# Value products and modulation steps that start with their last operand, and experts turned in pairs

## The chip, the cores and the metric

The kernel runs as one program on one core of a Trainium2 chip. The time is the device time of one execution in microseconds (us). TensorE (PE in the profile) multiplies, VectorE (DVE) and ScalarE (ACT) work elementwise, GpSimd (POOL) helps with a few small operations, and SyncE (SP) issues all DMAs on one queue. Each engine takes its instructions in the order in which they stand in its program.

## The reference, cut to what matters

Two transformer layers over 256 latent and 256 context tokens, with D = 1024. Each layer has a modulation, four attention branches and a channel mixer. Layer 0 has a dense SwiGLU, layer 1 eight experts of which each token takes two:

```
m = silu(cond) @ w_mod[l] + b_mod[l]                 # shift, scale and gate of both halves of a layer
p = softmax(q @ k.T * scale);  out = p @ v           # branches a, b, d; c subtracts two softmaxes
for each expert e and its tokens t:
    y[t] += w[t, e] * ((silu(h[t] @ w1[e]) * (h[t] @ w3[e])) @ w2[e])
x = x + m_gate * y
```

## The kernel before

**Layout.** Activations lie feature-major. Matrices are split into a float32r high and low part and multiplied in three float32r passes (`mm3`, L280). Plain float32 products also occur; each of these is two instructions in the trace. Three kinds of product use only part of TensorE's 128 columns at a time and put several results beside each other in different columns.

**Modulation (L310).** `mod_group` handles one of 40 background steps. It loads four tiles of `wmod`, then issues eight float32 products of 32 columns each: for k = 0 the four column groups g = 0 to 3, then for k = 1 the same. The last tile to land, `w[3]`, is read by k = 1, g = 2 and 3. In the trace a step is 16 instructions, L317.

**Value products (L625 to L632).** In the branches a, b and d a pair of heads gets its scores, an Exp, a division and transposes (L613); ScalarE copies the transposes into `both[0]` and `both[1]` (L615). Then `o[64j:64j+64]` sums V times `both[j]` over the key blocks, j = 0 before j = 1, each in 64 of the 128 columns. `turned` is the last of the copies, that of `both[1]`. There are 36 such products: 24 with four key blocks (16 instructions in the trace) and 12 with two (8 instructions), all L630.

**Experts (L1323 to L1346).** Per expert there are seven chunks of 512 hidden features. `gate_up` (L1410) multiplies up to 96 gathered tokens with four pieces of 1 MB each, in 72 products of 32 columns (`acc<-wraw,xg`, L1405 to L1408); ScalarE and VectorE form silu(gate)*up in the tile `ga`. `turn` (L1433) transposes it in three instructions (L1438) and copies it to `aT`. `down` (L1443) multiplies `aT` with two more pieces into `S` (36 products). The loop issues gate_up of chunk c, down of chunk c-1, turn of chunk c. At each expert's second chunk `selection` (L1224) makes a weighted selection matrix in two VectorE instructions, two transposes (L1231) and a copy. After the next expert's first chunk `weigh` (L1243) copies the expert's result to `ysb`, and `combine` (L1258) multiplies it with the weighted selection in eight float32 products (L1266, 16 instructions); VectorE adds these to the sum (L1355). Every second expert `gather` (L1234) collects tokens for two experts.

**Loading.** `pieces` (L1365) lists the 336 pieces in the order of use. They rotate through 8 + 5 + 4 = 17 buffers (`R1`, `R2` and two tiles that were `hh` and `hl`). A buffer is loaded again when its last product is done.

**Order.** The order on each engine is set by a scheduler that plays the program through with its own estimates of durations (L1622). It puts next on an engine what it holds to be ready. `issue_after(x)` puts those instructions of a block that run on x's own engine behind x; around the value products x is a ScalarE copy, and the block holds TensorE products alone.

Of the kernel before, what the change touches and what calls it, by code (L numbers as in the profile page):

```python
# [10 lines left out]
F32 = mybir.dt.float32  # L11
# [35 lines left out]
class Prog:  # L47
# [262 lines left out]
    def mod_group(self, l, G, s):  # L310

        nc = self.nc
        ps = self.acc()
        w = self.wloads(self.I["wmod"][l, 4 * G + s], 2048, self.mod_ring)
        for k in range(2):
            for g in range(4):
                nc.tensor.matmul(ps[32 * g:32 * g + 32, 0:256], self.sc[:, 2 * s + k, :],  # L317
                                 w[2 * k + g // 2][:, 256 * (g % 2):256 * (g % 2) + 256], start=k == 0, stop=k == 1)
# [252 lines left out]
    def attn_pair(self, qts, keys, smm, br, V, sink=None, mask=False, diff=False):  # L571


        nc = self.nc
        k0, nk = keys
        n = 128 * nk
        nq = len(qts)
        c0 = 128 * qts[0]
        hi, lo = br[0][:, c0:c0 + 128 * nq], br[1][:, c0:c0 + 128 * nq]
        oall = self.acc("tp") if diff else None  # L580
        both = None if diff else [self.at.tile([128, 4, 256], F32, name="PT2", tag="PT", bufs=self.PTB)[:, :nk] for _ in range(2)]
        for qi, qt in enumerate(qts):
            st = self.sm.tile([128, 8], F32, name="st", tag="st", bufs=6)
            P = []
            for j in range(2):
                S = self.acc("S")[:, :n]
                smm(S, j, qt)
                if mask and qt < 2:
                    ob = slice(128, 256) if qt == 0 else slice(0, 128)
                    nc.vector.tensor_tensor(S[:, ob], S[:, ob], self.amask[qt], op=OP.add)  # L590
                nm = st[:, j:j + 1]
                nc.vector.tensor_reduce(nm, S, axis=AX.X, op=OP.max, negate=True)
                if sink is not None:
                    nc.vector.tensor_scalar(nm, nm, self.nsink[:, sink + j:sink + j + 1], None, op0=OP.min)
                p = self.at.tile([128, 512], F32, name="P", tag="P", bufs=self.PB)[:, :n]
                nc.scalar.activation(p, S, AF.Exp, bias=nm, accum_out=st[:, 2 + j:3 + j])
                P.append(p)
            if sink is not None:
                nc.gpsimd.tensor_tensor(st[:, 4:6], self.sink[:, sink:sink + 2], st[:, 0:2], op=OP.add)
                nc.scalar.activation(st[:, 4:6], st[:, 4:6], AF.Exp)  # L600
                nc.vector.tensor_tensor(st[:, 2:4], st[:, 2:4], st[:, 4:6], op=OP.add)
            nc.vector.reciprocal(st[:, 2:4], st[:, 2:4])
            if diff:
                nc.vector.tensor_scalar(P[1], P[1], st[:, 3:4], self.lam, op0=OP.mult, op1=OP.mult)
                nc.vector.scalar_tensor_tensor(P[0], P[0], st[:, 2:3], P[1], op0=OP.mult, op1=OP.subtract)
            else:
                for j in range(2):
                    nc.vector.tensor_scalar(P[j], P[j], st[:, 2 + j:3 + j], None, op0=OP.mult)
            PT = []
            for j in range(1 if diff else 2):  # L610
                tp = self.acc("tp")
                for kc in range(nk):
                    nc.tensor.transpose(tp[:, 128 * kc:128 * kc + 128], P[j][:, 128 * kc:128 * kc + 128], self.ident)  # L613
                if not diff:
                    turned = nc.scalar.copy(both[j][:, :, 128 * qi:128 * qi + 128], tp[:, :n].rearrange("p (k t) -> p k t", t=128))  # L615
                    continue
                pt = self.at.tile([128, 4, 256], F32, name="PT", tag="PT", bufs=self.PTB).rearrange("p k t -> p (k t)")[:, :n]
                self.evac(pt, tp[:, :n])
                PT.append(pt)
            if diff:  # L620
                for kc in range(nk):
                    self.last_pv = nc.tensor.matmul(oall[:, 128 * qi:128 * qi + 128], PT[0][:, 128 * kc:128 * kc + 128],
                                     V(k0 // 128 + kc, 0), start=kc == 0, stop=kc == nk - 1)
                continue
        if not diff:  # L625
            o = self.acc("tp")[:, :128 * nq]
            with self.tc.issue_after(turned.ins):
                for kc in range(nk):
                    for j in range(2):
                        nc.tensor.matmul(o[64 * j:64 * j + 64], V(k0 // 128 + kc, j), both[j][:, kc, :],  # L630
                                         start=kc == 0, stop=kc == nk - 1)
# [592 lines left out]
    def selection(self, selT, pos, w, n=CAP):  # L1224
# [6 lines left out]
            nc.tensor.transpose(tp[0:n, 128 * t:128 * t + 128], sw, self.ident)  # L1231
        nc.scalar.copy(selT, tp[0:n, 0:256])

    def gather(self, htok, sel, n, put):  # L1234

        for k in range(KC):
# [21 lines left out]
    def combine(self, part, put):  # L1258

        nc = self.nc  # L1260
        ysb, selT = part
        for i in range(4):
            c = self.acc("tp")
            for j in range(2):
                dc = 2 * i + j
                nc.tensor.matmul(c[:, 256 * j:256 * j + 256], ysb[:, 128 * dc:128 * dc + 128], selT, start=True, stop=True)  # L1266
            put(i, c.rearrange("p (j t) -> p j t", j=2))

    def moe(self, x, close):
# [4 lines left out]
        with self.pool("epm") as self.ep:  # L1274
            with self.tc.issue_after(self.last_pow.ins):
                self.route_consts()
            R1, R2 = 8, 5
            self.loaded = []
            self.order = self.pieces()
            self.rings = [(self.ep, "wraw", R1, 1)] * R1  # L1280
# [6 lines left out]
            with self.pool("spm", side="right") as self.ex:  # L1287
# [16 lines left out]

                def chosen(e):

                    sel = self.ex.tile([128, 2, 2, CAP], F32R, name="sel", tag="sel", bufs=1)
# [11 lines left out]
                    return xg  # L1319

                xg = chosen(0)
                prev = None
                for e in range(NE):  # L1323
                    if e and e % 2 == 0:
                        xg = nxt
                    for c in range(7):
                        with self.tc.issue_after(self.last_tok.ins) if e == 0 else nullcontext():
                            a = self.gate_up(xg, CAP * (e % 2))
                            if prev:
                                self.down(*prev)  # L1330
                            prev = c, self.turn(a)
                            if e == 0 and c == 1:
                                rest()
                        if c == 0 and e:
                            self.combine(self.weigh(self.y, selT), lambda i, v: self.add_to(macc, i, v, e == 1))
# [5 lines left out]
                self.down(*prev)  # L1341
# [23 lines left out]
    def pieces(self):  # L1365


        out, prev = [], None
        for e in range(NE):
            for c in range(7):  # L1370
                out += [self.I["w13"][e, c, h] for h in range(4)]
                if prev:
                    out += [self.I["w2"][prev[0], prev[1], h] for h in range(2)]
                prev = e, c
        return out + [self.I["w2"][prev[0], prev[1], h] for h in range(2)]

    def load_next(self):

# [31 lines left out]
    def gate_up(self, xg, c0):  # L1410
# [9 lines left out]
        a = self.ex.tile([128, MAIN], F32, name="ga", tag="ga", bufs=2)  # L1420
# [12 lines left out]
    def turn(self, a):  # L1433
# [5 lines left out]
        aT = self.ex.tile([128, 3, 128], F32, name="aT", tag="aT", bufs=2)  # L1439
# [187 lines left out]
```

## Time and profile before

| | |
|---|---|
| median of 3 runs | 2608.15 us (2607.58 to 2610.31) |
| the profiled execution's own time | 2609.64 us |
| its span, first to last instruction | 2607.9 us |
| TensorE busy | 2564.9 us, 98% |
| VectorE, ScalarE, GpSimd busy | 46%, 36%, 4% |
| mean granted TensorE clock | 0.993 of full speed |
| experts, about 1623 us to the end | DMA moves 340 to 400 GB/s |

Busy time counts a column group that works alone as busy too, so a busy TensorE can still be working with half of its columns. Whether it does is seen in the timeline: what one start is later than the last.

### The profile page before, as it was taken

To read this page: it belongs to the slowest core of one execution; us is meant where nothing else is said; L and a number is where in the kernel's file an instruction comes from. 1 tells how busy PE (TensorE), PEld (TensorE's weight loads), DVE (VectorE), ACT (ScalarE), POOL (GpSimd) and SP (SyncE) were. 2 spreads that over 40 slices of the span, in tenths; PEclk is the share of its full clock that TensorE was granted. 3 is DMA by queue.
4 is the path that set the end of the run, shared out by engine and by line. 5 is a ranking of instruction groups with operands and counts; after the bars stand their busy time and mean duration, and the time that the engine had idled before them with its cause. 6 is when DMAs were issued, how large, how long until landed. Compare 5 with 4: busy or idle time off the path is not lost.

```text
span 2607.9 us, 54549 instructions
## 1 busy us (share of the span) xinstructions
PE 2564.9 (98%) x22762; PEld 1986.3 (76%) x22762; DVE 1212.5 (46%) x2820; ACT 929.6 (36%) x2179; POOL 116.5 (4%) x118
## 2 busy tenths in 40 slices
PE   8999999999999999999999999999999999999998
PEld 6866788898788778888888998666666666666665
DVE  6767666557574434458777786111112121211121
ACT  4556556444443323336666664111111111111111
POOL 0111010000000000001210001000000000000000
PEclk9999999999999999999999999999999999999999
DMA  6423321222352352345442457998898999898992
GB/s 239 130 72 94 107 90 65 82 75 91 97 170 69 110 173 95 89 128 173 148 130 86 138 160 293 405 393 353 342 378 350 362 363 378 359 359 350 397 360 81
DMA packets 153467, 543.22 MB, mean 208 GB/s; under 512 B 17920, under 2 KB 25216, under 8 KB 109696
## 3 DMA queue, kind: packets, MB, share of 16 engines
q1 hardware_dynamic: 153216, 539.68, 56.6%
q8 instruction: 181, 2.97, 0.4%
q14 instruction: 70, 0.57, 0.1%
HBM read 538.57 MB, written 1.05 MB: 207 GB/s over the span
## 4 chain that ended last, share of the span: by engine, by line


## 5 line engine op out<-in xcount | busy, mean ns | idle before, releaser
L1405 PE MATMUL acc<-wraw,xg 128*32 128x384 f32 x5376 | 606.8, 487 | 0.0
L1406 PE MATMUL acc<-wraw,xg 128*32 128x256 f32 x1792 | 471.8, 380 | 0.0
L260 ACT CAST whi<-wraw 128x512 fp32r<-128x512 f32 (+2 forms) x484 | 293.0, 608 | 453.8 <-PE acc L283 261.8
L261 DVE TENSOR_TENSOR wlo<-wraw,whi 128x512 fp32r<-128x512 f32 (+2 forms) x484 | 323.7, 672 | 275.1 <-ACT whi L260 267.6
L1429 DVE SCALAR_TENSOR_TENSOR ga<-ga,acc 96x192 f32<-96x192 f32 x224 | 79.6, 355 | 670.8 <-ACT ga L1427 666.5
L1405 PE MATMUL S<-wraw,aT 128*32 128x384 f32 x2688 | 306.3, 486 | 0.6 <-ACT aT L1440 0.6
L1405 PEld LDWEIGHTS acc<-wraw,xg 128*32 128x32 f32 x5376 | 224.1, 110 | 73.1 <-issue 12.0
L1427 ACT ACTIVATE ga<-acc 96x192 f32<-96x192 f32 x224 | 72.9, 326 | 547.5 <-PE acc L1408 544.9
L1408 PE MATMUL acc<-wraw,xg 128*32 128x256 f32 x896 | 266.5, 379 | 0.0
L1406 PE MATMUL S<-wraw,aT 128*32 128x256 f32 x896 | 239.2, 379 | 0.0
L1406 PEld LDWEIGHTS acc<-wraw,xg 128*32 128x32 f32 x1792 | 190.7, 110 | 59.2
L283 PE MATMUL acc<-wlo,hh 128*128 128x256 f32 (+1 forms) x752 | 212.6, 284 | 0.0
L284 PE MATMUL acc<-whi,hl 128*128 128x256 f32 (+1 forms) x752 | 212.1, 284 | 0.0
L282 PE MATMUL acc<-whi,hh 128*128 128x256 f32 (+1 forms) x752 | 210.9, 284 | 0.1
L282 PE MATMUL acc<-hh,whi 128*128 128x256 f32 (+1 forms) x616 | 209.2, 341 | 0.6 <-DVE tg L882 0.6
L284 PE MATMUL acc<-hh,wlo 128*128 128x256 f32 (+1 forms) x616 | 208.5, 339 | 0.0
L283 PE MATMUL acc<-hl,whi 128*128 128x256 f32 (+1 forms) x616 | 207.0, 337 | 0.0
L255 POOL TENSOR_TENSOR rs_y<-rs_x,half 128x8 f32<-128x8 f32 (+3 forms) x64 | 100.6, 1577 | 1336.6 <-DVE rs_x L254 1294.5
L282 PEld LDWEIGHTS acc<-whi,hh 128*128 128x128 f32 x752 | 140.4, 188 | 5.9 <-issue 3.2
L283 PEld LDWEIGHTS acc<-wlo,hh 128*128 128x128 f32 x752 | 141.5, 188 | 3.1 <-issue 1.6
L284 PEld LDWEIGHTS acc<-whi,hl 128*128 128x128 f32 x752 | 141.1, 188 | 2.0 <-DVE hl L422 0.4
L1408 PEld LDWEIGHTS acc<-wraw,xg 128*32 128x32 f32 x896 | 98.6, 110 | 55.1
(360 smaller groups left out, 4952.2 us busy)
## 6 DMA issues: line engine op xcount, KB each, us to landing
wraw<-w SPq DMA_DIRECT2D x336, 1024.0 KB, 7.5
wraw<-wmod SPq DMA_DIRECT2D x192, 256.0 KB, 3.8
wraw<-wgate SPq DMA_DIRECT2D x128, 256.0 KB, 2.8
wraw<-wq SPq DMA_DIRECT2D x112, 256.0 KB, 3.6
wraw<-wff SPq DMA_DIRECT2D x88, 256.0 KB, 2.8
wraw<-wbr SPq DMA_DIRECT2D x64, 256.0 KB, 2.8
wraw<-wout SPq DMA_DIRECT2D x32, 256.0 KB, 2.9
wraw<-wfd SPq DMA_DIRECT2D x32, 256.0 KB, 2.7
```

Source lines behind the costliest of these rows:

```text
L255: self.last_pow = self.nc.gpsimd.tensor_tensor(y, x, self.half[:, :n], op=OP.pow)
L260: return (self.nc.scalar.copy(hi, src), self.nc.vector.tensor_tensor(lo, src, hi.bitcast(F32), op=OP.subtract))
L261: self.nc.vector.tensor_tensor(lo, src, hi.bitcast(F32), op=OP.subtract))
L282: mm(out, a[0], b[0], start=start, stop=False, **kw)
L283: mm(out, a[0], b[1], start=False, stop=False, **kw)
L284: self.last_mm = mm(out, a[1], b[0], start=False, stop=stop, **kw)
L1405: mm(out[j][32 * i:32 * i + 32, 0:MAIN], lhs(i), w[:, MAIN * j:MAIN * j + MAIN], start=start, **kw)
L1406: mm(out[j][CAP:128, 0:REST], lhs(2 * j), r, start=start, **kw)
L1408: mm(out[0][CAP:128, REST:2 * REST], lhs(1), r, start=False, **kw)
L1427: nc.scalar.activation(t, g, AF.Tanh, scale=0.5)
L1429: nc.vector.scalar_tensor_tensor(t, t, 1.0, g, op0=OP.add, op1=OP.mult)
```

## The change

Four edits. The modulation's eight products begin with those that read the tile that lands last (k = 1 before 0, g = 2 and 3 before 0 and 1). The value products begin with j = 1, and `issue_after(turned)` is gone. The experts' loop keeps two fresh gate_up results, turns both in a row, and runs `down` two chunks behind; `aT` gets four buffers, `ga` three, the ring 16 pieces in place of 17, and `pieces` follows the new order. For the first seven experts the weighted selection is replaced: `slot_weights` transposes the 0/1 selection matrix of the gather and gets each slot's weight from two float32 products of one column; `weigh_parts` scales the copied result by that weight and splits it in a float32r high and low part, and `combine` multiplies both parts with the selection in float32r. The last expert is combined as before.

```diff
-        for k in range(2):
-            for g in range(4):
+        for k in (1, 0):
+            for g in (2, 3, 0, 1):
                 nc.tensor.matmul(ps[32 * g:32 * g + 32, 0:256], self.sc[:, 2 * s + k, :],
-                                 w[2 * k + g // 2][...], start=k == 0, stop=k == 1)
+                                 w[2 * k + g // 2][...], start=k == 1, stop=k == 0)
...
-            with self.tc.issue_after(turned.ins):
-                for kc in range(nk):
-                    for j in range(2):
-                        nc.tensor.matmul(o[64 * j:64 * j + 64], V(k0 // 128 + kc, j), both[j][:, kc, :],
+            for kc in range(nk):
+                for j in (1, 0):
+                    nc.tensor.matmul(o[64 * j:64 * j + 64], V(k0 // 128 + kc, j), both[j][:, kc, :],
...
+    def slot_weights(self, sel, e):
+        tp = self.acc("tp")
+        for t in range(2):
+            nc.tensor.transpose(tp[0:CAP, 128 * t:128 * t + 128], sel[:, t, e % 2, :].bitcast(F32), self.ident)
+        selT = self.ex.tile([CAP, L], F32R, name="selT", tag="selT", bufs=2)
+        nc.scalar.copy(selT, tp[0:CAP, 0:256])
+        ps = self.acc("tp")
+        for t in range(2):
+            nc.tensor.matmul(ps[0:CAP, 0:1], sel[:, t, e % 2, :].bitcast(F32), self.wt[:, t, e:e + 1], start=t == 0, stop=t == 1)
+        w = self.ex.tile([CAP, 1], F32, name="sw", tag="slw", bufs=2)
+        nc.vector.tensor_copy(w, ps[0:CAP, 0:1])
+        return selT, w
+
+    def weigh_parts(self, y, part):
+        selT, w = part
+        ysb, _ = self.weigh(y, selT)
+        hi, lo = (self.ex.tile([CAP, 1024], F32R, name=n, tag=n, bufs=1) for n in ("yhi", "ylo"))
+        nc.scalar.activation(hi, ysb, AF.Copy, scale=w)
+        nc.vector.scalar_tensor_tensor(lo, ysb, w, hi.bitcast(F32), op0=OP.mult, op1=OP.subtract)
+        return (hi, lo), selT
...
-                nc.tensor.matmul(c[...], ysb[:, 128 * dc:128 * dc + 128], selT, start=True, stop=True)
+                v = ysb if isinstance(ysb, tuple) else (ysb,)
+                for h, u in enumerate(v):
+                    nc.tensor.matmul(c[...], u[:, 128 * dc:128 * dc + 128], selT, start=h == 0, stop=h == len(v) - 1)
...
-            R1, R2 = 8, 5
+            R1, R2 = 8, 4
...
-                            a = self.gate_up(xg, CAP * (e % 2))
+                            fresh.append((c, self.gate_up(xg, CAP * (e % 2))))
+                            done = None
                             if prev:
-                                self.down(*prev)
-                            prev = c, self.turn(a)
+                                done = prev.pop(0)
+                                self.down(*done)
+                            if len(fresh) == 2:
+                                prev, fresh = [(c, self.turn(a)) for c, a in fresh], []
...
-                        if c == 0 and e:
-                            self.combine(self.weigh(self.y, selT), ...)
-                        if c == 1:
+                        if e and done and done[0] == 6:
+                            self.combine(self.weigh_parts(self.y, part), ...)
+                        if c == 2 and e < NE - 1:
+                            part = self.slot_weights(self.sel, e)
+                        elif c == 2:
...
```

TensorE's program at a value product of branch d, in layer 0 (`PT` is `both`: 2688 is j = 0, 2689 is j = 1; `br` belongs to a background product). Before:

```order
L284 MATMUL acc<-br_1490,wlo 128x512
L630 MATMUL tp<-PT_2688,V 64x256
L282 MATMUL acc<-br_1492,whi 128x512
L283 MATMUL acc<-br_1493,whi 128x512
L284 MATMUL acc<-br_1492,wlo 128x512
L630 MATMUL tp<-PT_2689,V 64x256
L630 MATMUL tp<-PT_2688,V 64x256
```

After the change the same product, with the same background work ahead of it:

```order
L283 MATMUL acc<-br_1493,whi 128x512
L284 MATMUL acc<-br_1492,wlo 128x512
L629 MATMUL tp<-PT_2689,V 64x256
L629 MATMUL tp<-PT_2688,V 64x256
L629 MATMUL tp<-PT_2689,V 64x256
L629 MATMUL tp<-PT_2688,V 64x256
```

The first product of j = 0 stood alone, three background products ahead of the rest; now nothing stands between. Over the program, 28 of the 36 value products had such a lone first product; now none is broken.

TensorE's program where an expert is combined (`acc<-wraw,xg` is the next expert's gate_up). Before:

```order
L1405 MATMUL acc<-wraw,xg 32x384 x2
L1266 MATMUL tp<-selT,ysb 128x256 x4
L1405 MATMUL acc<-wraw,xg 32x384
L1406 MATMUL acc<-wraw,xg 32x256
L1408 MATMUL acc<-wraw,xg 32x256
L1405 MATMUL acc<-wraw,xg 32x384
L1266 MATMUL tp<-selT,ysb 128x256 x2
```

After the change, the first two of three stretches:

```order
L1438 MATMUL acc<-wraw,xg 32x384 x2
L1292 MATMUL tp<-selT,yhi 128x256 x3
L1438 MATMUL acc<-wraw,xg 32x384
L1439 MATMUL acc<-wraw,xg 32x256
L1441 MATMUL acc<-wraw,xg 32x256
L1438 MATMUL acc<-wraw,xg 32x384 x3
L1292 MATMUL tp<-selT,ylo 128x256
L1292 MATMUL tp<-selT,yhi 128x256
L1292 MATMUL tp<-selT,ylo 128x256 x2
```

Eight float32 products became sixteen in float32r, in three stretches before (4, 2, 2) and after (3, 9, 4). They now begin 29 rows of products into a gate_up of 72, where they began after 11.

TensorE's program from a `down` over the turn to the next gate_up, before:

```order
L1406 MATMUL S<-wraw,aT 32x256
L1438 MATMUL tp<-cst,ga 128x128 x3
L1405 MATMUL acc<-wraw,xg 32x384 x3
```

After:

```order
L1439 MATMUL S<-wraw,aT 32x256
L1471 MATMUL tp<-cst,ga 128x128 x6
L1438 MATMUL acc<-wraw,xg 32x384 x3
```

Six transposes stand together at every second chunk. Where no turn stands, gate_up follows a `down` directly.

## Rows read from the trace of the kernel before

**Rows 1.** The page: each engine's busy time, share and instructions.

```profile
PE 2564.9 (98%) x22762; PEld 1986.3 (76%) x22762; DVE 1212.5 (46%) x2820; ACT 929.6 (36%) x2179; POOL 116.5 (4%) x118
```

**Rows 2.** Waits of PE: line <- releaser: us in total, times, longest us.

```profile
PE acc L317 <- DMA wraw<-wmod: 1.9, 4, 1.1
...
PE tp L630 <- ACT PT L615: 0.4, 1, 0.4
```

**Rows 3.** PE's timeline at a broken value product: start us, us, engine, line, operation, count.

```profile
239.30 0.65 PE L630 MATMUL tp<-PT,V 128*64 128x256 f32 x2
239.88 0.50 PE L282 MATMUL acc<-br,whi 128*128 128x512 f32 x1
240.22 0.40 PE L283 MATMUL acc<-br,whi 128*128 128x512 f32 x1
240.45 0.40 PE L284 MATMUL acc<-br,wlo 128*128 128x512 f32 x1
240.78 1.94 PE L630 MATMUL tp<-PT,V 128*64 128x256 f32 x14
242.65 0.55 PE L613 MATMUL tp<-cst,P 128*128 128x128 f32 x3
```

**Rows 4.** PE's timeline at a value product that is not broken.

```profile
398.38 1.95 PE L630 MATMUL tp<-PT,V 128*64 128x256 f32 x16
400.26 0.66 PE L613 MATMUL tp<-cst,P 128*128 128x128 f32 x4
```

**Rows 5.** PE's timeline at a piece of a modulation step and at a whole one.

```profile
405.28 0.62 PE L317 MATMUL acc<-wraw,sc 128*32 128x256 f32 x2
405.83 0.65 PE L613 MATMUL tp<-cst,P 128*128 128x128 f32 x4
...
903.11 1.07 PE L317 MATMUL acc<-wraw,sc 128*32 128x256 f32 x16
904.11 0.50 PE L282 MATMUL acc<-act,whi 128*128 128x512 f32 x1
```

**Rows 6.** PE's timeline from one turn of an expert's chunk to the next.

```profile
1981.45 0.55 PE L1438 MATMUL tp<-cst,ga 128*128 128x128 f32 x3
...
1996.79 0.50 PE L1405 MATMUL S<-wraw,aT 128*32 128x384 f32 x3
...
1997.11 0.50 PE L1405 MATMUL S<-wraw,aT 128*32 128x384 f32 x3
...
1997.61 0.55 PE L1438 MATMUL tp<-cst,ga 128*128 128x128 f32 x3
1998.08 0.52 PE L1405 MATMUL acc<-wraw,xg 128*32 128x384 f32 x3
```

**Rows 7.** PE's timeline in the chunk after, where an expert is combined.

```profile
2000.14 1.99 PE L1266 MATMUL tp<-selT,ysb 96*128 96x256 f32 x8
...
2003.05 1.13 PE L1266 MATMUL tp<-selT,ysb 96*128 96x256 f32 x4
...
2019.60 0.55 PE L1438 MATMUL tp<-cst,ga 128*128 128x128 f32 x3
```

**Rows 8.** PE's timeline in a stream of float32r products of 256 columns.

```profile
465.02 0.28 PE L283 MATMUL acc<-wlo,hh 128*128 128x256 f32 x1
...
465.60 0.28 PE L282 MATMUL acc<-whi,hh 128*128 128x256 f32 x1
```

**Rows 9.** Groups by line: float32 products of one column (busy us, mean ns).

```profile
L392 PE MATMUL tp<-ones,sacc 128*128 128x1 f32 x16 | 2.0, 229 | 0.0
```

**Rows 10.** ScalarE's timeline at an expert's result.

```profile
1997.28 2.14 ACT L293 COPY ysb<-S 96x384 f32<-96x384 f32 x5 [3.83 <-PE S L1408]
```

**Rows 11.** Groups by line: ScalarE's copies for the value products, and a VectorE subtraction.

```profile
L615 ACT COPY PT<-tp 128x512 f32<-128x512 f32 x96 | 54.2, 589 | 25.0 <-PE tp L613 24.8
...
L261 DVE TENSOR_TENSOR wlo<-wraw,whi 128x512 fp32r<-128x512 f32 x438 | 299.9, 688 | 243.7 <-ACT whi L260 236.4 <-ACT Q L503 2.6 <-PE acc L284 1.6
```

**Rows 12.** Windows: length, busy us of each engine, PE clock, DMA share, GB/s.

```profile
1650.00:1700.00 50.00, 50.00 (x680) 34.04 (x676) 9.57 (x30) 5.75 (x16) 0.00 (x0) 1.00 0.99 400
```

More of the change, by code (lines that the diff above doesn't have):

```diff
@@ L314, in mod_group @@
         w = self.wloads(self.I["wmod"][l, 4 * G + s], 2048, self.mod_ring)
-        for k in range(2):
-            for g in range(4):
+        for k in (1, 0):
+            for g in (2, 3, 0, 1):
                 nc.tensor.matmul(ps[32 * g:32 * g + 32, 0:256], self.sc[:, 2 * s + k, :],
-                                 w[2 * k + g // 2][:, 256 * (g % 2):256 * (g % 2) + 256], start=k == 0, stop=k == 1)
+                                 w[2 * k + g // 2][:, 256 * (g % 2):256 * (g % 2) + 256], start=k == 1, stop=k == 0)
         self.mod_flush()
@@ L614, in attn_pair @@
                 if not diff:
-                    turned = nc.scalar.copy(both[j][:, :, 128 * qi:128 * qi + 128], tp[:, :n].rearrange("p (k t) -> p k t", t=128))
+                    nc.scalar.copy(both[j][:, :, 128 * qi:128 * qi + 128], tp[:, :n].rearrange("p (k t) -> p k t", t=128))
                     continue
@@ L626, in attn_pair @@
             o = self.acc("tp")[:, :128 * nq]
-            with self.tc.issue_after(turned.ins):
-                for kc in range(nk):
-                    for j in range(2):
-                        nc.tensor.matmul(o[64 * j:64 * j + 64], V(k0 // 128 + kc, j), both[j][:, kc, :],
-                                         start=kc == 0, stop=kc == nk - 1)
+            for kc in range(nk):
+                for j in (1, 0):
+                    nc.tensor.matmul(o[64 * j:64 * j + 64], V(k0 // 128 + kc, j), both[j][:, kc, :],
+                                     start=kc == 0, stop=kc == nk - 1)
             self.split(hi, lo, o)
@@ L1232, in selection @@
         nc.scalar.copy(selT, tp[0:n, 0:256])
+    def slot_weights(self, sel, e):
+        nc = self.nc
+        tp = self.acc("tp")
[10 more added lines that the diff above has]
+    def weigh_parts(self, y, part):
+        nc = self.nc
+        selT, w = part
[4 more added lines that the diff above has]
+        return (hi, lo), selT
     def gather(self, htok, sel, n, put):
@@ L1265, in combine @@
                 dc = 2 * i + j
-                nc.tensor.matmul(c[:, 256 * j:256 * j + 256], ysb[:, 128 * dc:128 * dc + 128], selT, start=True, stop=True)
+                v = ysb if isinstance(ysb, tuple) else (ysb,)
+                for h, u in enumerate(v):
+                    nc.tensor.matmul(c[:, 256 * j:256 * j + 256], u[:, 128 * dc:128 * dc + 128], selT, start=h == 0, stop=h == len(v) - 1)
             put(i, c.rearrange("p (j t) -> p j t", j=2))
@@ L1305, in chosen @@
                 def chosen(e):
-                    sel = self.ex.tile([128, 2, 2, CAP], F32R, name="sel", tag="sel", bufs=1)
+                    sel = self.sel = self.ex.tile([128, 2, 2, CAP], F32R, name="sel", tag="sel", bufs=1)
                     with self.tc.issue_after(self.last_tok.ins) if e == 0 else nullcontext():
@@ L1321, in moe @@
                 xg = chosen(0)
-                prev = None
+                prev, fresh = [], []
                 for e in range(NE):
@@ L1327, in moe @@
                         with self.tc.issue_after(self.last_tok.ins) if e == 0 else nullcontext():
-                            a = self.gate_up(xg, CAP * (e % 2))
+                            fresh.append((c, self.gate_up(xg, CAP * (e % 2))))
+                            done = None
                             if prev:
-                                self.down(*prev)
-                            prev = c, self.turn(a)
+                                done = prev.pop(0)
+                                self.down(*done)
+                            if len(fresh) == 2:
+                                prev, fresh = [(c, self.turn(a)) for c, a in fresh], []
                             if e == 0 and c == 1:
                                 rest()
-                        if c == 0 and e:
-                            self.combine(self.weigh(self.y, selT), lambda i, v: self.add_to(macc, i, v, e == 1))
-                        if c == 1:
+                        if e and done and done[0] == 6:
+                            self.combine(self.weigh_parts(self.y, part), lambda i, v: self.add_to(macc, i, v, e == 1))
+                        if c == 2 and e < NE - 1:
+                            part = self.slot_weights(self.sel, e)
+                        elif c == 2:
                             selT = self.ex.tile([CAP, L], F32, name="selT", tag="selT", bufs=2)
@@ L1340, in moe @@
                             nxt = chosen(e + 1)
-                self.down(*prev)
+                for p in prev:
+                    self.down(*p)
                 for dc in range(KC):
@@ L1365, in pieces @@
     def pieces(self):
-        out, prev = [], None
+        out, prev = [], []
         for e in range(NE):
@@ L1371, in pieces @@
                 out += [self.I["w13"][e, c, h] for h in range(4)]
[L1372 to L1375, printed above, removed]
+                prev.append((e, c))
+                if len(prev) > 2:
+                    out += [self.I["w2"][(*prev[0], h)] for h in range(2)]
+                    prev.pop(0)
+        return out + [self.I["w2"][(*p, h)] for p in prev for h in range(2)]
     def load_next(self):
@@ L1419, in gate_up @@
                 self.slots(ps, lambda i: xg[:, k, c0 + 32 * i:c0 + 32 * i + 32], w[:, 1024 * j:1024 * j + 1024], k == 0, k == KC - 1)
-        a = self.ex.tile([128, MAIN], F32, name="ga", tag="ga", bufs=2)
+        a = self.ex.tile([128, MAIN], F32, name="ga", tag="ga", bufs=3)
         H = MAIN // 2
@@ L1438, in turn @@
             self.nc.tensor.transpose(tp[:, 128 * i:128 * i + 128], a[:, 128 * i:128 * i + 128], self.ident)
-        aT = self.ex.tile([128, 3, 128], F32, name="aT", tag="aT", bufs=2)
+        aT = self.ex.tile([128, 3, 128], F32, name="aT", tag="aT", bufs=4)
         self.nc.scalar.activation(aT.rearrange("p f s -> p (f s)"), tp[:, 0:MAIN], AF.Copy, scale=0.5)
```

## The prediction

> **What bounds the kernel now.** I read the page's busy times first: TensorE is busy 98% of the span, VectorE and ScalarE under half of it [rows 1]. Its table of waits is short: of 40 modulation steps four waited for their last load, 1.9 us in all, and of 36 value products one waited for a copy, 0.4 us [rows 2]. So the kernel takes as long as TensorE's list takes to run, and a gain must shorten that list. Busy time doesn't say how well the 128 columns are filled, so I went to the timeline next and looked at how much later one start is than the last. That shows two losses that count as busy: a product of 64 or 32 columns that stands alone, and the step into and out of a narrow layout. Last I read the experts in the same way, and their loads in the windows.
>
> **Sum, part by part.** Durations are of the profiled execution, 2609.6 us.
>
> *Value products.* In a stream of background products of 512 columns starts are 0.23 us apart; before a value product the step is 0.33, so the change of layout costs 0.10 [rows 3]. The lone first product of j = 0 holds TensorE from 239.30 to 239.88, 0.58, with half of the columns. The other 14 instructions take 240.78 to 242.65, 1.87. A product that is not broken takes 1.88 for all 16 [rows 4]: there the first j = 0 runs beside the first j = 1, and in the broken one that j = 1 runs with nothing beside it. So the lone piece is pure loss, 0.58 + 0.10 = 0.68. The program's order has 28 of them before and none after: 28 x 0.68 = **-19.0**. Below this the term can't be unless waits come (next but three); above it could be some us more, where background products stood badly too. Removing `issue_after(turned)` costs and gains nothing: it binds ScalarE's instructions, and the block has none.
>
> *Modulation steps.* A piece of two instructions holds TensorE 0.55, plus 0.10 for the layout: 0.65; a whole step of 16, which fills its four column groups evenly, 1.00 + 0.10 = 1.10 [rows 5]. With four groups of 32 columns, pieces of 2 to 8 instructions take about the same, since the fullest group sets it, and so do 10 to 16. Counted in the order: 40 stretches of up to 8 before and 21 after, 30 of 10 to 16 before and 35 after. -19 x 0.65 + 5 x 1.10 = **-6.9**. The order of the loads on SP's queue is that of the tiles and stays.
>
> *Turns.* In an expert's chunk the products of 384 columns start 0.32 apart (1996.79, 1997.11); over a turn the step is 1998.08 - 1997.11 = 0.97, so a turn costs 0.65 [rows 6]. Its three transposes and the way out take 0.47, so three more take at most 3 x 0.13. A pair costs 2 x 0.65 = 1.30 now and 0.65 + 0.36 = 1.0 then: 28 x -0.3 = -8.4. Four turns that were broken by a few gate_up products become one, some 0.2 each: **-9** together, -6 to -11. The chunk's period of 16.16 us (1981.45 to 1997.61) is otherwise kept: the same 108 products, none of them waiting for a copy, since at least a gate_up or a down lies between a tile's making and its use.
>
> *Combining.* In float32 four instructions more cost 1.99 - 1.13 = 0.86, 0.215 each [rows 7]; the float32r stream steps 0.58 in five, 0.116 each [rows 8]. Both have 16 instructions an expert, and three stretches. 7 x 16 x 0.10 = -11.1; a float32 stretch seems to start about 0.1 slower as well (1.13 for four is more than 0.86 and the end of one), of which I count half: **-12**, with ends 0 (float32r at 96 rows as slow as float32) and -15. The combining chunk now takes 2019.60 - 1997.61 = 22.0, 5.8 over a plain one, of which 3.4 is the products and the rest switching and badly filled columns; that rest I keep.
>
> ScalarE and VectorE stand ahead of it: five copies take 2.14 us for 1536 columns [rows 10], so the high part of 1024 takes about 1.4 and the low part, twice a subtraction of 512, also about 1.4 [rows 11]. The copies begin 0.3 before the last product of `down` ends (1997.28 against 1997.11 + 0.50), so the high part is there after some 3.2 us and the low one after 4.6. The program puts 29 of 72 gate_up rows ahead, 29/72 of two thirds of the chunk's 15.5, 4.2 us, and three to six rows and three products more before the low part: about 5.1. Cover, by 0.5 to 1 us; each us over would cost 7, as everything on TensorE queues behind. The selection's two VectorE steps fall away beside all this.
>
> *Slot weights.* Two transposes stay; two products of one column come, four instructions. At 2.0 us for 16 of such [rows 9] they are 0.5 us. At four experts they and the transposes have a stretch of their own, at three the products alone: 0.2 for both changes of layout, some 0.3 for unevenly filled columns. 7 x 1.0 = **+7**; ends +2 (four instructions for nothing) and +10 (0.23 each, the mean that the row gives).
>
> *New waits.* A product that starts with its last operand has it whole or waits with all of TensorE behind it. The scheduler goes by estimates, so I allow **+5**: 76 starts at under 0.1; ends 0 and 45 (below).
>
> Sum: -19.0 - 6.9 - 9 - 12 + 7 + 5 = -34.9, so 2609.6 becomes 2574.7. The median of the runs is 1.5 under the profiled execution, so **2573 us**.
>
> *A rule weighed.* The float32r stream steps 0.116 us, and each product in it has its own 128 columns of weights, so loads hide beside products [rows 8]. The Trainium skill, "TensorE: Matmul & The Clock Gate", part "The mechanism" under packing small matmuls, says that a weight load overlaps a running product only where the two use different row groups, and all of these use all rows. By its section on LDWEIGHTS 128 columns take about 107 ns, an estimate of that page; exposed, they would make a float32r step about 0.22 and the combining no cheaper. The row is against it.
>
> **The rivals.**
>
> 1. *Combining gains nothing.* At 96 rows with freshly written parts a float32r step may be no shorter than the 0.215 of float32. For: no row has float32r at 96 rows in this place. Against: [rows 8]. The -12 falls away: 2585. Chance 0.05.
>
> 2. *The experts' loads become the bound.* A pair of chunks takes 2 x 16.16 - 0.3 = 32.0 us and reads 12 MiB: 393 GB/s. The engines at a share of 0.99 moved 400 [rows 12], so 3% is left, and there is one buffer less. Against: all pieces are 352 MB for the experts' 970 us less 14, 368 GB/s, and 16 buffers hold 16 x 2.7 = 43 us of work. If loading holds the experts at the old pace, -14 of turns, combining and slots is lost: 2587. Chance 0.06.
>
> 3. *The wait takes the split's place, and the kernel is no faster.* Before, TensorE did half of a product's first pair or half of a modulation step while the copy or the last tile was on its way. Now it stands before 36 value products and 40 steps until the copy has landed. A copy takes 0.59 [rows 11]. At 76 x 0.46 = 35 us the gain is gone; at a whole copy each, 76 x 0.59 = 45, it is 2618, slower. For: TensorE takes nothing out of order. Against: the same copies and tiles were waited for before by the second operand, and this cost 2.3 us [rows 2]; and the program puts other work in front. Chance 0.05, of which 0.03 slower.
>
> **How the numbers follow.** My forecast has 0.84. With every bound at its good end (waits 0, combining -15, slots +2, turns -11) it is 2609.6 - 49.9 - 1.5 = 2558, the low end. At the bad end, waits +15, slots +10 and turns -6 give 2589, which takes in rivals 1 and 2: 2590. About 0.2% (5 us) is what a measurement of this kernel can tell from no change: faster 0.94, same 0.03, slower 0.03.
>
> **What would show it.** Right: no value product of two instructions with other products behind it, and each of 16 in 1.88; TensorE's start at the experts some 20 us earlier; pairs of chunks at 32.0 us; `yhi` and `ylo` at 0.116 a step. Wrong: waits at the value products or modulation steps above some 10 us; a wait for `yhi` or `ylo`; waits of gate_up for a load, with DMA at 0.99 throughout. The forecast is wrong if the part before the experts is not at least 12 us shorter.

## The result and the profile after

The changed kernel takes 2576.7 us (median of 4 runs, 2575.3 to 2578.0) against 2608.2 on the same chip: ratio 0.9878, 95% interval 0.9861 to 0.9895. That is 31.5 us less, where 35 were forecast (2573). The profiled executions differ by 32.0: spans of 2607.9 and 2575.9 us.

Where did they go? One row on each gather product tells when TensorE reaches the experts. First of the kernel before, then of the changed one: durations, and the start of the first and the last.

```profile
L1240 PE MATMUL acc<-sel,htok x128: 270/275/501, 1622.7 to 2320.4; 128*128 128x192 f32 x128
```

```profile
L1264 PE MATMUL acc<-sel,htok x128: 272/274/497, 1606.8 to 2289.2; 128*128 128x192 f32 x128
```

The layers became 1622.7 - 1606.8 = 15.9 us shorter, and what follows 32.0 - 15.9 = 16.1. The first was forecast at some 20, the second at 14.

**The layers.** The page's first line of the changed kernel answers to [rows 1]; below it its waits, which answer to [rows 2] (us in total, times, longest).

```profile
PE 2521.3 (98%) x22790; PEld 1982.5 (77%) x22790; DVE 1217.5 (47%) x2820; ACT 932.9 (36%) x2186; POOL 119.1 (5%) x118
```

```profile
PE acc L317 <- DMA wraw<-wmod: 7.9, 6, 2.4
PE S L667 <- ACT P L596: 6.7, 7, 1.4
...
PE tp L629 <- ACT PT L615: 1.6, 2, 1.2
```

The kernel before at its scores:

```profile
PE S L668 <- ACT P L596: 2.8, 6, 1.0
```

TensorE's share is the same 98%, but 43.6 us of busy time are gone, a loss that looked like work; 32.0 of them came off the span, and the other 11.6 came back as idle time. Modulation steps now wait 7.9 us for their last tile (1.9 before), value products 1.6 for the copy (0.4), and the scores 6.7 for a softmax (2.8). Next, TensorE's groups of the two edited lines: busy us, mean ns, idle us just before them and its releaser; the kernel before, then the changed one.

```profile
L630 PE MATMUL tp<-PT,V 128*64 128x256 f32 x480 | 79.8, 394 | 0.4 <-ACT PT L615 0.4
L317 PE MATMUL acc<-wraw,sc 128*32 128x256 f32 x640 | 60.6, 387 | 2.7 <-DMA wraw<-wmod 1.9 <-DVE wlo L261 0.7
```

```profile
L629 PE MATMUL tp<-PT,V 128*64 128x256 f32 x480 | 61.5, 395 | 1.7 <-ACT PT L615 1.6
L317 PE MATMUL acc<-wraw,sc 128*32 128x256 f32 x640 | 52.9, 391 | 8.6 <-DMA wraw<-wmod 7.9 <-DVE merged L881 0.8
```

Instructions are as many and as long as before; only how many run side by side has changed. The value products take 18.3 us less and wait 1.3 more: -17.0. The modulation steps take 7.7 less and wait 5.9 more: -1.8. Two value products in TensorE's timeline answer to [rows 3, 4].

```profile
200.62 3.68 PE L629 MATMUL tp<-PT,V 128*64 128x256 f32 x16 [1.18 <-ACT PT L615]
204.23 2.27 PE L613 MATMUL tp<-cst,P 128*128 128x128 f32 x8
...
237.48 1.95 PE L629 MATMUL tp<-PT,V 128*64 128x256 f32 x16
239.35 0.39 PE L282 MATMUL S<-K,Qd 96*128 96x256 f32 x1
```

At 237.48, where [rows 3] had a lone pair and 14 more, all 16 take 1.87, as forecast. The one at 200.62 waited 1.18 for its copy and then took 3.61. A window shows why (its length, then each engine's busy time with its instructions, granted clock, DMA share, GB/s).

```profile
199.90:206.70 6.80, 5.84 (x24) 3.15 (x24) 1.37 (x5) 2.88 (x11) 0.00 (x0) 0.50 0.00 0
```

The granted clock is 0.50, the lower of its two levels (1.2 GHz). It fell at 199.9, within that wait; just ahead of it TensorE had also stood 1.41 and 1.30 us for softmaxes of the scores (until 195.80 and 198.06), so the copy alone is not shown to have cost it. Two modulation steps close together show the same (answering to [rows 5]).

```profile
1141.41 1.06 PE L317 MATMUL acc<-wraw,sc 128*32 128x256 f32 x12
1143.17 0.61 PE L392 MATMUL tp<-ones,sacc 128*128 128x1 f32 x4 [0.71 <-DVE sacc L384]
1145.09 1.70 PE L317 MATMUL acc<-wraw,sc 128*32 128x256 f32 x16 [1.31 <-DMA wraw<-wmod]
1146.72 0.58 PE L282 MATMUL acc<-fh,hh 128*128 128x256 f32 x1
1147.10 0.42 PE L283 MATMUL acc<-fl,hh 128*128 128x256 f32 x1
1147.32 0.42 PE L284 MATMUL acc<-fh,hl 128*128 128x256 f32 x1
...
1149.05 0.28 PE L282 MATMUL acc<-fh,hh 128*128 128x256 f32 x1
1149.16 0.28 PE L283 MATMUL acc<-fl,hh 128*128 128x256 f32 x1
```

```profile
1145.40:1148.80 3.40, 3.40 (x25) 2.38 (x18) 2.87 (x10) 1.95 (x4) 0.29 (x1) 0.50 0.50 145
```

TensorE stood 0.71 and 1.31 us; then the step takes 1.63 instead of 1.00, and the float32r products behind it stand 0.21 apart, until they are 0.12 again. So a wait can cost more than its row in the table. It need not: behind the longest wait for a tile the granted clock stayed at 1.00, and the step took 1.00.

```profile
1212.02 1.07 PE L317 MATMUL acc<-wraw,sc 128*32 128x256 f32 x16 [2.41 <-DMA wraw<-wmod]
1213.02 0.66 PE L613 MATMUL tp<-cst,P 128*128 128x128 f32 x4
```

Of the six waits for a tile only that at 1145.09 was followed by half clock. Nor is half clock new: the kernel before has 10.2 us of it from 177.3, and the mean granted clock over the span is 0.993 in both kernels. So it explains single slow products, and hardly anything of the difference between the kernels. The Trainium skill, "TensorE: Matmul & The Clock Gate", section "HAM oscillation — how this bites in real kernels", describes waits for data, some 3 to 5 us each in its example, that send the engine back to half its clock, so that the work behind starts slow. The two stretches above agree with it in kind, with shorter waits (1.41, 1.30 and 1.18 us; 0.71 and 1.31), and in this trace the length of one wait alone does not decide it: 2.41 us passed without a fall.

**The experts.** Three pairs of turns, answering to [rows 6, 7].

```profile
1940.18 0.87 PE L1471 MATMUL tp<-cst,ga 128*128 128x128 f32 x6
...
1972.20 0.87 PE L1471 MATMUL tp<-cst,ga 128*128 128x128 f32 x6
...
1995.30 0.28 PE L1292 MATMUL tp<-selT,yhi 96*128 96x256 f32 x1
1995.42 0.40 PE L1292 MATMUL tp<-selT,ylo 96*128 96x256 f32 x2
1995.65 0.28 PE L1292 MATMUL tp<-selT,yhi 96*128 96x256 f32 x1
1995.77 0.39 PE L1292 MATMUL tp<-selT,ylo 96*128 96x256 f32 x2
1995.99 0.28 PE L1292 MATMUL tp<-selT,yhi 96*128 96x256 f32 x1
1996.11 0.28 PE L1292 MATMUL tp<-selT,ylo 96*128 96x256 f32 x1
...
2008.20 0.87 PE L1471 MATMUL tp<-cst,ga 128*128 128x128 f32 x6
...
2011.50 0.49 PE L1438 MATMUL acc<-wraw,xg 128*32 128x384 f32 x1
2011.92 0.50 PE L1243 MATMUL tp<-z,sel 128*96 128x1 f32 x4
2012.35 0.52 PE L1438 MATMUL acc<-wraw,xg 128*32 128x384 f32 x2
...
2041.50 0.77 PE L1471 MATMUL tp<-cst,ga 128*128 128x128 f32 x5
```

A plain pair takes 1972.20 - 1940.18 = 32.02, forecast at 32.0. The pair that combines takes 36.00, 3.98 more, where the combining chunk of [rows 7] was 5.8 over a plain one. The combining steps stand 0.116 apart (1996.11 - 1995.30 = 0.81 in seven). The pair behind it, 33.30 long, holds an expert's slot weights: 1.28 over a plain one.

### The profile page after: what moved, and what is told of

Same layout as the page of the kernel before. It is cut to its first block, busy times and chain, and to the rows that moved or that the text cites. A ratio compares the mean times of both kernels' runs of the same rounds, so it can differ in the third digit from the quotient of the medians.

```text
span 2575.9 us, 54553 instructions
## 1 busy us (share of the span) xinstructions
PE 2521.3 (98%) x22790; PEld 1982.5 (77%) x22790; DVE 1217.5 (47%) x2820; ACT 932.9 (36%) x2186; POOL 119.1 (5%) x118
## 4 chain that ended last, share of the span: by engine, by line
## 5 line engine op out<-in xcount | busy, mean ns | idle before, releaser
L1438 PEld LDWEIGHTS acc<-wraw,xg 128*32 128x32 f32 x5376 | 229.0, 110 | 54.6 <-issue 5.6
L1439 PEld LDWEIGHTS acc<-wraw,xg 128*32 128x32 f32 x1792 | 191.9, 110 | 66.5
L1441 PEld LDWEIGHTS acc<-wraw,xg 128*32 128x32 f32 x896 | 98.6, 110 | 58.7
```

Of the source, the lines that this page charges most:

```text
L1438: mm(out[j][32 * i:32 * i + 32, 0:MAIN], lhs(i), w[:, MAIN * j:MAIN * j + MAIN], start=start, **kw)
L1439: mm(out[j][CAP:128, 0:REST], lhs(2 * j), r, start=start, **kw)
L1441: mm(out[0][CAP:128, REST:2 * REST], lhs(1), r, start=False, **kw)
```

## The experiments

Each time is a median, and beside it the difference from the kernel before in runs on the same chip; the changed kernel's own is -31.5. Intervals of the ratios are about 0.0015 to either side (4 us) with four runs.

**Value products alone**, on the kernel before: j = 1 first and `issue_after` gone, both as in the diff of the change.

> The kernel before with the value products' new order alone (j = 1 first, `issue_after` gone). Theory: the 28 lone first pairs go, 28 x 0.68 = 19.0 us, less 1 to 2 us of waits for the second copy: 2590 (2588 to 2592), and the time to the experts' first gather product 17 to 19 shorter. Rival (the wait takes the place of the split): 2600 or more, with waits for PT above 5 us at these products. Second rival (the gain came from background work falling better in the changed kernel as a whole): under 12 us here.

2597.9 (-11.6; 0.9954, 0.9939 to 0.9969): no more than two thirds of what was expected, and just within what the second rival gave. The experts are reached at 1612.3, 10.4 us earlier, where 17 to 19 were expected. Its rows of the two lines and of the scores' wait:

```profile
L629 PE MATMUL tp<-PT,V 128*64 128x256 f32 x480 | 61.2, 394 | 3.1 <-ACT PT L615 3.1
L317 PE MATMUL acc<-wraw,sc 128*32 128x256 f32 x640 | 61.4, 387 | 4.9 <-DMA wraw<-wmod 3.3 <-DVE st L592 1.4 <-DVE merged L881 0.2
```

```profile
PE S L667 <- ACT P L596: 6.1, 6, 1.4
```

At their own line the products gain what the theory says: 18.6 of busy time less 2.7 more of waits, -15.9. But the modulation line has 3.0 more (61.4 + 4.9 against 60.6 + 2.7), and the scores wait 3.3 more. This fits a scheduler that places the other work anew around stretches that can no longer be cut, so that other instructions meet operands that are not ready; no run tests that reading.

**The modulation's order alone**, on the kernel before.

```diff
-        for k in range(2):
-            for g in range(4):
+        for k in (1, 0):
+            for g in (2, 3, 0, 1):
```

> The kernel before with the modulation steps' new order alone. Theory after the comparison of the two traces: the packing of 40 short pieces into fewer gains 4 to 7 us, and waits of the first instruction for the last wmod tile, 5 to 7 us, give it back: 2605 to 2610, the same as before, with more than 5 us of waits at L317. Rival (the prediction's own term, waits small): 2601. Rival (the waits outweigh the packing): 2612 or more.

2615.6 (+6.2; 1.0024, 1.0015 to 1.0033): slower, the last rival. Its group at L317:

```profile
L317 PE MATMUL acc<-wraw,sc 128*32 128x256 f32 x640 | 54.9, 392 | 7.5 <-DMA wraw<-wmod 6.9 <-DVE rawq L471 0.6
```

Busy 5.7 us less, idle 4.8 more: by itself a draw, as the theory had it. So the loss lies elsewhere. 3.7 is at the scores, which wait 6.5 for their softmax (2.8 before). And 2.9 of the 7.0 between the profiled executions lies behind the first gather product (at 1626.8), where nothing was changed; the windows around it show the granted clock (the third number from the end), first of this kernel, then of the one before:

```profile
1600.00:1700.00 100.00, 94.39 (x1063) 71.75 (x1066) 31.80 (x97) 20.35 (x47) 0.72 (x1) 0.91 0.94 383
```

```profile
1600.00:1700.00 100.00, 94.39 (x1123) 70.77 (x1125) 30.10 (x94) 19.26 (x45) 0.72 (x1) 0.95 0.98 400
```

Behind the first gather product the lower level lasts 10.5 us (to 1637.3) here and 5.2 (to 1627.9) in the kernel before: 5.3 more, which cost 2.6 us of full-speed time, nearly all of the 2.9. Why the clock was low for longer in this run is not known.

**The experts' edits alone** (both layer edits put back).

> The changed kernel with both layer edits (value products, modulation steps) put back, so the experts' edits alone. Theory: the experts' 16.5 us, 2591.5 (2590 to 2593), with the part before the experts as long as before. Rival (the experts gained because they began earlier, with other loads in the buffers): over 2597.

2593.1 (-16.3; 0.9937, 0.9922 to 0.9952). The experts are reached at 1622.9, as before. So the two halves of the change add: -16.3 and, for both layer edits together, 31.5 - 16.3 = 15.2 by difference (15.9 in the traces). Run singly, the two layer edits gave -11.6 and +6.2, no more than -5.4 together.

**The modulation's order put back** in the changed kernel (the diff of the second experiment, reversed).

> The changed kernel with only the modulation steps' order put back. Theory (packing and waits cancel): 2574 to 2579 against 2576.7 of the changed kernel, waits for wmod at L317 back at about 2 us instead of 7.9. Rival (the prediction's term of -6.9 holds, and the time was lost elsewhere in the layers): 2583. Rival (the order costs more than it gains): 2572 or less.

2582.8 (-26.6; 0.9896, 0.9881 to 0.9912), 5 to 6 us over the changed kernel: the rival. Beside whole value products the new order gains about what the prediction gave it; alone it lost 6.2. With the value products whole and the old order the list has 72 rows of modulation products, with the new one 57; on the kernel before it was 71 and 60. That is four rows more of packing (15 against 11), too little for a difference of 11 us, of which the clock behind the layers made 3. Up to the experts this kernel's TensorE list is that of the first experiment, yet its profiled execution reaches them at 1615.6 and that one at 1612.3; it alone has 10.2 us at half clock, from 1289.3. So some 3 us between two traces can be the clock. Why the two orders help each other stays open; the intervals of this kernel and the changed one overlap in part.

**Float32 combining and weighted selection back**, pairs kept.

```diff
-                        if c == 2 and e < NE - 1:
-                            part = self.slot_weights(self.sel, e)
-                        elif c == 2:
+                        if c == 2:
...
-                            self.combine(self.weigh_parts(self.y, part), ...
+                            self.combine(self.weigh(self.y, selT), ...
```

> The changed kernel with the float32 combining and the weighted selection put back, pairs of chunks kept: what the combining and the slot weights are worth together. Theory (combining -1.77 us an expert by its pairs, slot weights +1.0): 2576.7 + 12.4 - 6.8 = 2582 (2580 to 2584), with the chunk pair that combines back at some 37.8 us and no stretch of slot weights. Rival (the prediction's first: the combining gained nothing and the pairs brought everything): 2576.7 less 6.8, 2570. Second rival (the slot weights ate all of it): 2577.

2583.3 (-26.8; 0.9896, 0.9879 to 0.9912): 5 to 7 over the changed kernel, as the theory had it. The pair that combines, from turn to turn:

```profile
1972.95 0.87 PE L1469 MATMUL tp<-cst,ga 128*128 128x128 f32 x6
...
2010.82 0.88 PE L1469 MATMUL tp<-cst,ga 128*128 128x128 f32 x6
```

37.87 against 36.00: the float32r combining is 1.87 an expert, 13.1 if all seven gain as much. In three of the seven the same pair holds the slot weights too, and there it is 37.53 against 37.08, 0.45 for both together. From the first gather product (at 1606.7 here) to the end the three kernels take 985.2 (before), 974.1 (this one) and 969.1 us (the changed one): the pairs with all that goes with them brought 11.1, combining and slot weights together 5.0. The first rival is out.

**Buffers given back earlier.** A step's last two tiles take the buffers of the step before's first two, and the new order reads those last.

```diff
-        for k in (1, 0):
-            for g in (2, 3, 0, 1):
+        for q in (3, 0, 1, 2):
+            k = q // 2
+            for g in (2 * (q % 2), 2 * (q % 2) + 1):
...
```

> The changed kernel with the tiles of a modulation step in the order last, first, second, third (3, 0, 1, 2) in place of 3, 2, 1, 0. A step still begins with the tile that lands last, but the first two tiles, whose buffers the next step's last two tiles take, are given back earlier (of 16 instructions after 8 and 12, not after 16 and 12). Theory (the waits come from buffers given back late): waits for wmod at L317 (here L318) fall by 0.5 us for each of the six waits, from 7.9 to about 5, time 2573 to 2576. Rival (the waits are the loads' own latency, wherever the buffer comes free): no change in the waits, 2576.7 within 2. Rival (any order that begins with the last tile does the same, and what differs between kernels is chance of the schedule): a change of more than 3 us in either sign, not at L317.

2578.0 (-32.0; 0.9873, 0.9857 to 0.9890), and the wait is no shorter:

```profile
PE acc L318 <- DMA wraw<-wmod: 9.1, 6, 2.5
```

Three other kernels here whose layers are those of the changed kernel wait 8.1, 8.4 and 9.1 us for these tiles, so 9.1 isn't longer either. The theory in this form falls: a few tenths of a microsecond at the buffers don't show.

**Half of the load left out.**

```diff
-        w = self.wloads(self.I["wmod"][l, 4 * G + s], 2048, self.mod_ring)
+        w = self.wloads(self.I["wmod"][l, 4 * G + s], 1024, self.mod_ring)
...
-                                 w[2 * k + g // 2][:, ...
+                                 w[k][:, ...
```

> The changed kernel with half of each modulation step's load left out: two tiles of 512 columns are loaded and each is read by eight products, so the number of products and of stretches stays, but six buffers hold three steps; half of the modulation's weights don't enter. Theory (the new order waits because the next step's last tiles find no free buffer until the step before has ended): waits for wmod at L317 fall from 7.9 to under 2 us, with them the stretches of half clock that follow them, and the time to 2566 to 2571. Rival (the waits don't come from the buffers): waits above 5 us, 2574 or more.

2564.3 (-45.8; 0.9819, 0.9803 to 0.9836), more than expected. No wait for a tile is left; the step that waited 1.31 us in the changed kernel now follows the one ahead of it without a break, 28 instructions in one:

```profile
L317 PE MATMUL acc<-wraw,sc 128*32 128x256 f32 x640 | 53.2, 386 | 0.5 <-DVE merged L881 0.5
```

```profile
1136.57 0.70 PE L409 MATMUL S<-dg,ones 128*128 128x256 f32 x2
1137.19 1.92 PE L317 MATMUL acc<-wraw,sc 128*32 128x256 f32 x28
1139.05 0.38 PE L282 MATMUL acc<-fh,hh 128*128 128x256 f32 x1
```

**The old order with half of the load.**

> As e9 (half of each modulation step's load left out, half of the modulation's weights don't enter), but with the modulation steps' old order. In the program's order this has 60 rows of modulation products against 57 of e9, where with whole loads it is 72 against 57. Theory (both the short pieces of the old order and the waits of the new one come from the last tiles being late; with the tiles in time the order hardly matters): 2564.3 + 3 x 0.65 = 2566 (2563.5 to 2568). Rival (the new order packs by itself, loads or not): 2571 or more.

2570.6 (-39.4; 0.9853, 0.9836 to 0.9869): between the two expectations, nearer to the rival's. In place the theory holds:

```profile
L317 PE MATMUL acc<-wraw,sc 128*32 128x256 f32 x640 | 54.7, 386 | 0.5 <-DVE merged L881 0.5
```

With the tiles in time the old order has 54.7 us of busy time, not 60.6 to 62.7 as with whole loads, and 24 stretches of up to 8 instructions, not 40: it is hardly cut into pieces any more. So late tiles made the waits of the new order and most of the extra busy time of the old one. But the new order is worth 6.3 us here, as much as with whole loads (5 to 6), and only 1.5 of it is in this row: the rest stays open, and in time the rival is not out.

**Buffers of their own** for a step's last two tiles in layer 1.

```diff
-        w = self.wloads(self.I["wmod"][l, 4 * G + s], 2048, self.mod_ring)
+        own = self.mod_ring and self.mod_ring[1] == "mw"
+        w = [self.wload(..., 512, self.mod_ring if not own or q in (2, 3) else None) for q in range(4)]
...
+            if l == 1:
+                self.mod_ring = self.bp, "mw", 3
...
```

> The changed kernel, where in layer 1 the last two tiles of each modulation step have three buffers of their own (6 KB a partition that stand free in that layer), the first two stay in the six shared ones; whole computation. Theory (the waits are buffers given back late; a step's last tiles can then be asked for while the step before still runs): waits for wmod at L317 (here L318) fall from 7.9 to 2 to 5 us, and the stretches at half clock that follow them with them; 2568 to 2574. Rival (the shared queue of loads is late as a whole, so buffers change nothing): waits over 7 us, 2576 or more.

2577.2 (-32.7; 0.9874, 0.9857 to 0.9890): no gain, though the wait reads 4.9 us in three.

```profile
PE acc L318 <- DMA wraw<-wmod: 4.9, 3, 2.2
```

The last experiment has the same TensorE list up to the experts, and there the wait is 6.8 us in six: how far own buffers shorten it is not sure. What makes the tiles late, buffers or the one queue that asks for all loads in order, is thus not settled: half the load takes away both.

**Fewer buffers for the experts' loads**, 12 instead of 16 (`R1, R2 = 6, 2`).

> The changed kernel with 12 buffers of 1 MB for the experts' loads in place of 16 (R1, R2 = 6, 2); TensorE's list is the same, row for row. Theory (loads don't bound the experts: in the trace of the changed kernel each lands at least some 28 us before its use, and four buffers are 4 x 2.7 = 11 us): 2576.7 within 1.5, no wait of gate_up or down for a load. Rival (the prediction's second: loading is near the bound, and each buffer less costs): waits for the loads at L1438, 2582 or more.

2575.6 (-33.7; 0.9870, 0.9854 to 0.9887), and gate_up and down never wait for a load: the prediction's second rival is out.

**Slot weights at a turn.** They move to the chunk with the turn, and the one-column products go into the transposes' bank.

```diff
-                        if c == 2 and e < NE - 1:
+                        if c == 3 - e % 2 and e < NE - 1:
...
-        ps = self.acc("tp")
-            nc.tensor.matmul(ps[0:CAP, 0:1], ...
+            nc.tensor.matmul(tp[0:CAP, 256:257], ...
...
```

> The changed kernel with the slot weights moved to the chunk after which a turn stands anyway (c = 3 for even experts, c = 2 for odd), and the one-column products written beside the transposes in one bank, so that turn, transposes and products are one stretch of full-array work in all seven experts. Theory (of the 1.28 and 1.08 us that slot weights cost an expert, about 0.6 is the change of layout and unfilled columns): 7 x 0.6 = 4 us less, 2572.5 (2571 to 2574.5). Rival (the four one-column instructions themselves cost it): 2576 or more.

2573.2 (-36.9; 0.9859, 0.9842 to 0.9875), the best of the versions with the whole computation. By its time alone it can't be told from the changed kernel, but the rows can:

```profile
2006.85 0.87 PE L1470 MATMUL tp<-cst,ga 128*128 128x128 f32 x6
...
2007.77 0.42 PE L1240 MATMUL tp<-z,sel 128*96 128x1 f32 x4
2008.12 0.52 PE L1437 MATMUL acc<-wraw,xg 128*32 128x384 f32 x3
...
2039.34 0.87 PE L1470 MATMUL tp<-cst,ga 128*128 128x128 f32 x6
```

The pair takes 32.49 instead of 33.30: slot weights cost 0.47 where they cost 1.28. The instructions are the same; 0.8 was the stretch of its own (chunk and bank were changed together). From the first gather product to the end the kernel takes 964.8 us against 969.1.

**Both together** (this and the own buffers).

> The changed kernel with the slot weights at the turn (as e7) and the own buffers for the modulation's last tiles (as e11): the version that should beat both. Theory (the two gains lie in different parts of the program and add): e11 less 3.5 us, 2565 to 2571. Rival (they don't add, or e11 gains nothing): 2573 or more.

2574.2 (-35.7; 0.9864, 0.9848 to 0.9881): the rival; the buffers add nothing.

## Why the prediction was right, and where it was not

It was right in its main steps; the gain came 3.5 us smaller, and the waits and the modulation steps were mis-sized. That the layers came out near the sum is in part luck: singly its two layer edits gave -11.6 and +6.2, where it had -19.0 and -6.9, and it has no term for what they do to each other.

- *Value products.* -19.0 forecast; 18.3 of busy time went, and 22 of the 24 products of 16 take 1.87 or 1.88, as forecast; the other two ran in part at half clock. Their waits took 1.3 back. That removing `issue_after(turned)` does nothing holds: with that alone removed, the program that is built is the same.
- *Modulation steps.* -6.9 forecast, -7.7 of busy time measured, but 5.9 of waits came at the same line. The step that failed was to count the packing and leave the lateness of the tiles to a general allowance: a piece was cut because its last tile was late, and a whole step then waits for it. By the prediction's own test (waits above some 10 us at these two lines) it stands on the border: 9.5 for tiles and copies, 10.3 with all idle time at the two lines.
- *New waits.* +5 forecast. At the two edited lines there are 1.2 + 6.0 = 7.2 more, and 3.9 at the scores, where none was looked for: 11.1. With these, -18.3 - 7.7 + 11.1 = -14.9, where 15.9 was measured. Ahead of the experts TensorE's busy time fell by 27.4 in all and its idle time rose from 32.9 to 44.4 us, by 11.5. The third rival (35 to 45) had the mechanism at too high a price for the whole kernel. For the modulation steps it all but holds at their own line (-1.8), though with the old order put back the kernel took 5 to 6 us longer.
- *Turns.* 16.16 x 2 - 32.02 = 0.30 a pair: 28 x 0.30 = -8.4 of the -9, as forecast.
- *Combining.* -12 forecast, 1.87 an expert measured where it stands alone (7 x 1.87 = -13.1), at 0.116 a step as [rows 8] has it. `yhi` takes 1.15 and `ylo` 1.28 us, and TensorE waits for neither. The rule of the Trainium skill that was weighed ("TensorE: Matmul & The Clock Gate", "The mechanism"), by which a float32r step would be about 0.22, an estimate, doesn't hold at 96 rows either.
- *Slot weights.* +7 forecast. 1.28 an expert where they have a stretch of their own, of which the selection before had 0.22 (the last expert still makes it, and its pair takes 32.24): about 1 each. Together with the combining they come to 5.0 less, where -12 + 7 = -5 was forecast.
- *Loads.* No wait, and four buffers less change nothing.

The experts' 16.1 are thus 11.1 for the pairs and 5.0 for combining and slot weights. Of the 11.1, 8.4 are the turns; the other 2.7 must lie in the chunks that were broken or that gather, and were not taken apart.

## What to carry to other kernels

A busy engine can hide a wait as half-filled work. Where a product is cut because one operand is late, an order that begins with the late operand removes the cut, but the lateness stays: count it at that line as a wait, and look first at what would make the operand earlier. Measure such an order beside the edits that it will live with: the same one lost 6.2 us alone and gained 5 to 6 beside the other. Small products that force a change of layout belong beside work that has their layout already: that was worth some 0.8 us each time.

## What was not expected of the hardware

Behind waits of 1.41, 1.30 and 1.18 us, and behind 0.71 and 1.31, the granted clock stood at 0.50 for 6.8 and 3.4 us, in which 16 products took 3.61 and 1.63 instead of 1.87 and 1.00; behind a wait of 2.41 us it stayed at 1.00. And four one-column products cost 0.43 in a stretch of their own, but 0.35 behind transposes, the way out of the layout included in both.
